# Seven-product row pairs in an fp32 decoder trunk: sums ahead of low parts on VectorE, and four of eight row pairs by seven products in the second MLP matrices and in retention's gates and values

## The chip, the cores and the metric

The kernel runs on one NeuronCore of a Trainium2 chip. The metric is the device time of one execution in microseconds, lower is better. Before the change it was 2503.48 us (median of 3 runs, 2501.48 to 2504.06).

The engines are named as in the profile: PE (TensorE, matrix products), DVE (VectorE, elementwise work), ACT (ScalarE, casts, activations, copies out of PSUM), POOL (GpSimd, here mostly DMA issues), SP (SyncE, here the queue that issues the weight loads). Each runs its own instructions in the order of its own queue and waits for others by semaphores.

## The reference

A trunk of two layers on 256 tokens and a width of 2048, all in float32. Layer 0 is RetNet retention, layer 1 is multi-head latent attention (MLA); each is followed by a squared-ReLU MLP of width 8192.

```python
def retention(h, w_in, w_out, cos, sin):
    proj = h @ w_in
    q, k, v, gate = jnp.split(proj, [H * dk, 2 * H * dk, 2 * H * dk + H * dv], axis=-1)
    ...
    return (jax.nn.silu(gate) * o) @ w_out

def sq_relu_mlp(h, w1, w2):
    return jnp.square(jax.nn.relu(h @ w1)) @ w2

for layer in range(DEPTH):
    if layer < N_A_LAYERS:
        h = rms_norm(x, norm_mix[layer])
        x = x + retention(h, ret_w_in[layer], ret_w_out[layer], ret_cos, ret_sin)
    else:
        ...
        x = x + mla_attention(h, ...)
    x = x + sq_relu_mlp(rms_norm(x, norm_mlp[layer]), mlp_w1[layer], mlp_w2[layer])
```

Weights pass through the core once; nearly all work is products of 256 rows of activations with weight matrices.

## The kernel before, in words

**Split products.** PE multiplies in fp32r, a rounded format. To keep float32 accuracy every operand is split into a high part (the rounded value, a cast on ACT) and a low part (value minus high part, a subtraction on DVE): `split`, lines 183 and 184. A product of two operands is three matmuls into one PSUM bank: high by high (line 352), high by low of the weights (line 353), low by high (line 354).

**Row pairs.** `gemm_pair` multiplies the 256 activation rows by 1024 columns of a weight matrix. It walks over the 2048 contraction rows in eight row pairs of 256 rows, numbered 0 to 7; `quad` does one. One DMA on SP's queue brings 128x2048 elements (1 MB, tile `raw`, three buffers). They are four blocks of 128x512: b11, b22, b12, b21.

- *By eight products.* Two parts of 1024 elements are split; each part feeds four products. That is 24 matmuls, two casts and two subtractions of 1024.
- *By seven products* (the Strassen-Winograd form). Three adds on DVE (lines 312, 316, 317) make four sums of weight blocks in two tiles of 1024 (tag `us`, two buffers). Four parts are split: part 0 (b11 and b22, 1024), part 1 (b21, 512), part 2 (the second sums tile) and part 3 (the first). They feed 2, 1, 2 and 2 products: 21 matmuls. The activations need sums too (`with_sums`): three small operations on DVE and one more split of 512.

High and low parts of the weights live in tiles `wh` and `wl`, five buffers each, so casts and subtractions run at most a few parts ahead of PE.

**Which row pairs go by seven.** `SEVEN = (3, 5, 7)`; `FOUR = (3, 5, 6, 7)` and `QUERY = (3, 4, 6, 7)`. Before the change `FOUR` is used for the second half of MLA's output matrix (`wop`) and `QUERY` for MLA's query matrix (`dqp`). `SEVEN` is used for the first MLP matrices (`u`, without row pair 3 for the very first block), for the second MLP matrices (`d`), for retention's gates and values (`rp`, heads 1 to 7) and its output matrix (`ro`).

**The MLP.** Hidden width 8192 is taken in four groups of 2048. A group is two pairs of calls: two `gemm_pair` for w1 (a *u stage*), then two for w2 (a *d stage*, 1024 output columns each, called its first and second pair here). The result of the second u call is added up, squared, transposed and split while the first d pair already runs: function `up` in `mlp`, lines 778 to 800, which also calls `with_sums` for the hidden blocks whose index is in `SEVEN`. So the d stage's first pair shares its time with that work, and its second pair with `pair_out` of the first (lines 364 to 379) and with POOL's accumulating DMAs into x's home in DRAM (`to_home`, line 148). In each layer's last group the second pair is two plain `gemm` calls instead. That makes eight first pairs and six second pairs.

**Retention.** For heads 1 to 7, two projections (`rq`, `rk`) are followed by one `gemm_pair` (`rp`) for gate and value of the head. Its activations `act0` are the same for all heads; their sums are made once, in `first_inputs` (lines 571 to 586), from the tile `x0t`, which is kept until then.

**Order.** Python code runs once and emits instructions; the `later` list and `tick` decide where deferred work is emitted, and a scheduler then fixes the order of each engine's queue. Dependencies are tracked by tiles.

Of the kernel before, what the change touches and what calls it, by code (L numbers as in the profile page):

```python
# [11 lines left out]
F32 = mybir.dt.float32  # L12
# [3 lines left out]
AF = mybir.ActivationFunctionType  # L16
ALU = mybir.AluOpType
# [49 lines left out]
def yoco(ctx: ExitStack, tc: tile.TileContext, a):  # L67
# [86 lines left out]
    def gain(col):  # L154
        return gains[:, col : col + 1]
# [24 lines left out]
    def split(h, l, src, scale=None):  # L180

        if scale is None:
            nc.scalar.copy(h, src)  # L183
            nc.vector.tensor_tensor(l, src, h.bitcast(F32), op=ALU.subtract)  # L184
        else:
            nc.scalar.activation(h, src, AF.Copy, scale=scale)
            nc.vector.scalar_tensor_tensor(
                l, src, scale, h.bitcast(F32), op0=ALU.mult, op1=ALU.subtract
            )

    def split_act(v, src, scales=(None, None)):
        if scales == (None, None):
# [60 lines left out]
    def gemm_t(w, chunk0, act, nk, name, done):  # L253
# [3 lines left out]
        for g in range(n):  # L257
# [19 lines left out]

            stream(w, chunk0 + g, 2048, f"{name}{g}", use, (lambda: done(acc)) if g == n - 1 else None)

    def quad(w, chunk, x, mm, name):  # L280

        raw = pool.tile([P, 2048], F32, tag="raw", bufs=3, name=f"{name}_raw")
        nc.sync.dma_start(raw, w[chunk])
        v, more = x

        def a(t, k):
            return [v[:, k, i, t * P : (t + 1) * P] for i in range(2)]

        def s(n):
            return [more[:, n // 2, i, n % 2 * P : (n % 2 + 1) * P] for i in range(2)]  # L290

        def parts(src, n, part):
            wh = pool.tile([P, 1024], F32R, tag="wh", bufs=5, name=f"{name}_wh{part}")
            wl = pool.tile([P, 1024], F32R, tag="wl", bufs=5, name=f"{name}_wl{part}")
            split(wh[:, : n * 512], wl[:, : n * 512], src)
            return [[i[:, j * 512 : (j + 1) * 512] for i in (wh, wl)] for j in range(n)]

        if more is None:
            b11, b22 = parts(raw[:, 0:1024], 2, 0)
            mm("c11", a(0, 0), b11)  # L300
            mm("c21", a(1, 0), b11)
            mm("c12", a(0, 1), b22)
            mm("c22", a(1, 1), b22)
            b12, b21 = parts(raw[:, 1024:], 2, 1)
            mm("c12", a(0, 0), b12)
            mm("c22", a(1, 0), b12)
            mm("c11", a(0, 1), b21)
            mm("c21", a(1, 1), b21)
            return
        b11, b22 = parts(raw[:, 0:1024], 2, 0)  # L310
        u = [pool.tile([P, 2, 512], F32, tag="us", bufs=2, name=f"{name}_u{i}") for i in range(2)]
        nc.vector.tensor_tensor(
            u[0], raw[:, 0:1024].rearrange("p (i n) -> p i n", i=2),
            raw[:, 1024:1536].unsqueeze(1).to_broadcast([P, 2, 512]), op=ALU.add,
        )
        nc.vector.tensor_tensor(u[1][:, 0], u[0][:, 0], raw[:, 512:1024], op=ALU.add)
        nc.vector.tensor_tensor(u[1][:, 1], u[1][:, 0], raw[:, 1536:], op=ALU.add)  # L317
        mm("p1", a(0, 0), b11)
        mm("c12", s(3), b22)
        (b21,) = parts(raw[:, 1536:], 1, 1)  # L320
        mm("c11", a(0, 1), b21)
        u2, u4 = parts(u[1].rearrange("p i n -> p (i n)"), 2, 2)
        mm("c21", a(1, 1), u4)
        mm("p6", s(2), u2)
        u1, u3 = parts(u[0].rearrange("p i n -> p (i n)"), 2, 3)
        mm("p5", s(1), u1)
        mm("p7", s(0), u3)
# [243 lines left out]
    def first_inputs(c):  # L571

        t = f2k([2, S], f"x0t_{c}")
        nc.sync.dma_start(t, a["xt"][:, 2 * c : 2 * c + 2, :])
        v = act_tile(f"a0_{c}")
        split_act(v, t, [gain(G_MIX0 + 2 * c + j) for j in range(2)])
        act0.append(v)
        sums0.append(None)
        if c in SEVEN:

            def sum_up():
                for j in range(2):
                    nc.scalar.activation(t[:, j], t[:, j], AF.Copy, scale=gain(G_MIX0 + 2 * c + j))
                sums0[c] = with_sums(t, f"a0s_{c}")

            later(9 + c, sum_up)

# [140 lines left out]
    for h in range(RH):  # L728
        qk, gate, v, s = [], [], [], []
        if h == 0:  # L730

            def gated(acc, gate=gate):
                src = [f2k([512], f"gate_raw{t}") for t in range(NT)]
                for t in range(NT):
                    nc.scalar.copy(src[t], acc[t])

                def silu():
                    for t in range(NT):
                        g = f2k([512], f"gate0{t}")
                        nc.scalar.activation(g, src[t], AF.Silu, scale=r0[t])  # L740
                        gate.append(g)

                later(8, silu)

            gemm(a["ret_w_gv0"], 0, act0, KD, 512, "rg0", gated, start)
            ret_projected(h, qk, gate, v, s)
            gemm(
                a["ret_w_gv0"], 4, act0, KD, 512, "rv0",
                lambda acc, v=v, s=s, gate=gate: ret_valued(acc, 0, s, v, gate),
            )  # L750
            continue

        def paired(c, h=h, gate=gate, v=v, s=s):
            c = summed(c)
            for t in range(NT):
                nc.scalar.activation(c[t][0], c[t][0], AF.Silu, scale=r0[t])
                gate.append(c[t][0])
            ret_valued([c[t][1] for t in range(NT)], h, s, v, gate)

        ret_projected(h, qk, gate, v, s)  # L760
        if h == RH // 2:
            ret_out_half(0)
        need(r0, NT)
        while None in [sums0[k] for k in SEVEN]:
            run_first()
        gemm_pair(a["ret_w_gv"], (h - 1) * 8, list(zip(act0, sums0)), [k in SEVEN for k in range(8)], f"rp{h}", paired)
    ret_out_half(1)


    def mlp(layer, act, r, done):  # L770
        w1, w2 = a[f"mlp_w1_{layer}"], a[f"mlp_w2_{layer}"]
        f0 = 0
        for gi, nf in enumerate(GROUPS):
            hid, blocks = [], []
            kinds = [i in SEVEN for i in range(2 * nf)]
            last = gi == len(GROUPS) - 1

            def up(c, p, hid=hid, blocks=blocks):
# [7 lines left out]
                def turn(i):  # L786
                    for q in (2 * i, 2 * i + 1):
                        name = f"hid{layer}_{p}{q}"
                        tp = transposed(
                            lambda t, j: c[t][q // 2][:, (q % 2 * 2 + j) * P : (q % 2 * 2 + j + 1) * P], f"{name}_tp"  # L790
                        )
                        u = f2k([2, S], f"{name}_u")
                        nc.scalar.activation(u, tp, AF.Square)
                        v = act_tile(name)
                        split_act(v, u)
                        blocks.append((v, with_sums(u, name) if len(blocks) in SEVEN else None))
                        hid.append(v)

                later(0, lambda: turn(0))
# [382 lines left out]
```

## Time and profile before

| | |
|---|---|
| median of 3 runs | 2503.48 us |
| span of the profiled execution, first to last instruction | 2497.0 us |
| PEld (weight load) busy | 2075.1 us, 83% |
| POOL busy | 252.2 us, 10% |
| HBM traffic over the span | 207 GB/s |
| matmuls of `u`, `d`, `rp` from the activations themselves into c banks, on each of lines 352 to 354 | 748, 644, 322 |

The page's own execution spans 2497.0 us; some 6.5 us of the median lie outside of what the profile shows, or between runs. In the page a group's row gives count, busy time, the mean duration of one instruction, and the idle time of its engine just before such instructions with the engine that ended it. A window row gives each engine's busy time in a stretch. Busy time of overlapping instructions is counted once.

### The profile page before, as it was taken

The numbers are of one execution on the slowest core, as the hardware profiler recorded it, in microseconds if no ns is written. First come the engines' busy times: TensorE is split into PE (matmuls) and PEld (weight loads), VectorE is DVE, ScalarE is ACT, GpSimd is POOL, SyncE is SP. The second block draws the span as 40 slices with busy tenths as digits, with TensorE's granted clock in tenths as the row PEclk, the third lists the DMA queues.
The fourth block names the chain that finished last, engine by engine and source line by source line (L and its number), as shares of the span: only waits on it lengthen the run. The fifth ranks groups of instructions, "written<-read, shape, count | busy, mean of one in ns | idle before, by whom it ended". The sixth has DMA issues, their size and how long they took to land.

```text
span 2497.0 us, 31492 instructions
## 1 busy us (share of the span) xinstructions
PE 2471.9 (99%) x11683; PEld 2075.1 (83%) x11683; DVE 2096.7 (84%) x2723; ACT 1574.8 (63%) x2228; POOL 252.2 (10%) x308
## 2 busy tenths in 40 slices
PE   8999999999999999999999999999999999999999
PEld 7788888888888888888888888998888888888887
DVE  7788888888898888889889888776899888898896
ACT  6566555555676657566666767666676566575663
POOL 6300011000010110110110101110010201101100
PEclk9999999999999999999999999999999999999999
DMA  8545568555565685775875555444455956857754
GB/s 290 211 173 202 178 217 246 183 193 196 211 217 189 207 263 186 235 237 186 247 259 191 197 196 189 159 149 163 173 213 203 262 203 213 249 187 233 258 200 165
DMA packets 92825, 519.97 MB, mean 208 GB/s; under 512 B 11009, under 2 KB 12161, under 8 KB 39425
## 3 DMA queue, kind: packets, MB, share of 16 engines
q1 hardware_dynamic: 71280, 471.78, 52.5%
q0 software_dynamic: 21248, 46.15, 8.9%
q8 instruction: 91, 1.49, 0.2%
q14 instruction: 62, 0.50, 0.1%
q10 hardware_dynamic: 144, 0.05, 0.0%
HBM read 478.09 MB, written 39.85 MB: 207 GB/s over the span
## 4 chain that ended last, share of the span: by engine, by line
PE 80%; DVE 10%; DMA 4%; ACT 4%; issue 2%; POOL 1%; ACTq 0%; SPq 0%; DVEq 0%; POOLq 0%
PE u_c L353 7%; PE u_c L354 7%; PE u_c L352 7%; PE d_c L353 4%; PE d_c L354 4%; PE d_c L352 4%; PE rp_c L353 3%; PE rp_c L354 3%; PE rp_c L352 3%; DVE d_wl L184 3%; PE ro_c L352 2%; PE ro_c L353 2%; PE ro_c L354 2%; PE rq_acc L272 2%; PE rk_acc L272 2%; DMA d_raw<-in_mlp_w 2%
## 5 line engine op out<-in xcount | busy, mean ns | idle before, releaser
L184 DVE TENSOR_TENSOR u_wl<-u_raw,u_wh 128x1024 fp32r<-128x1024 f32 (+1 forms) x256 | 280.0, 1124 | 35.8 <-ACT u_wh L183 35.8
L184 DVE TENSOR_TENSOR d_wl<-d_raw,d_wh 128x1024 fp32r<-128x1024 f32 (+1 forms) x256 | 283.4, 1132 | 26.0 <-ACT d_wh L183 25.1
L353 PE MATMUL u_c<-u_wl,n 128*128 128x512 f32 x748 | 291.8, 390 | 1.1 <-DVE u_wl L184 1.0
L352 PE MATMUL u_c<-u_wh,n 128*128 128x512 f32 x748 | 291.3, 391 | 0.0
L354 PE MATMUL u_c<-u_wh,n 128*128 128x512 f32 x748 | 291.3, 389 | 0.0
L183 ACT CAST u_wh<-u_raw 128x1024 fp32r<-128x1024 f32 (+1 forms) x256 | 238.9, 981 | 60.6 <-DMA u_raw<-in_mlp_w 27.2
L183 ACT CAST d_wh<-d_raw 128x1024 fp32r<-128x1024 f32 (+1 forms) x256 | 240.0, 991 | 56.3 <-DMA d_raw<-in_mlp_w 25.1
L353 PE MATMUL d_c<-d_wl,hid 128*128 128x512 f32 x644 | 251.4, 390 | 1.7 <-DVE d_wl L184 1.6
L352 PE MATMUL d_c<-d_wh,hid 128*128 128x512 f32 x644 | 252.1, 391 | 0.0
L354 PE MATMUL d_c<-d_wh,hid 128*128 128x512 f32 x644 | 250.9, 390 | 0.0
L183 ACT CAST u_wh<-u_u 128x1024 fp32r<-128x1024 f32 x92 | 94.2, 1050 | 153.5 <-DVE u_u L317 129.8
L183 ACT CAST d_wh<-d_u 128x1024 fp32r<-128x1024 f32 x84 | 84.9, 1049 | 162.6 <-DVE d_u L317 154.7
L353 PEld LDWEIGHTS u_c<-u_wl,n 128*128 128x128 f32 x748 | 140.5, 188 | 31.1 <-DVE u_wl L184 2.8
L354 PEld LDWEIGHTS u_c<-u_wh,n 128*128 128x128 f32 x748 | 140.4, 188 | 29.2
L352 PEld LDWEIGHTS u_c<-u_wh,n 128*128 128x128 f32 x748 | 140.4, 188 | 28.6
L183 ACT CAST rp_wh<-rp_raw 128x1024 fp32r<-128x1024 f32 x112 | 106.7, 972 | 67.7 <-PE rp_c L354 37.5
L184 DVE TENSOR_TENSOR u_wl<-u_u,u_wh 128x1024 fp32r<-128x1024 f32 x92 | 110.7, 1222 | 43.6 <-ACT u_wh L183 43.5
L353 PEld LDWEIGHTS d_c<-d_wl,hid 128*128 128x128 f32 x644 | 120.9, 188 | 29.0 <-DVE d_wl L184 4.5
L354 PEld LDWEIGHTS d_c<-d_wh,hid 128*128 128x128 f32 x644 | 120.9, 188 | 25.1
L352 PEld LDWEIGHTS d_c<-d_wh,hid 128*128 128x128 f32 x644 | 120.9, 188 | 24.6
L184 DVE TENSOR_TENSOR d_wl<-d_u,d_wh 128x1024 fp32r<-128x1024 f32 x84 | 99.9, 1222 | 35.9 <-ACT d_wh L183 35.9
L148 POOL DMA_DIRECT2D xh<-d_c x48 | 42.1, 1029 | 844.6 <-ACT d_c L369 844.5
(567 smaller groups left out, 6570.0 us busy)
## 6 DMA issues: line engine op xcount, KB each, us to landing
u_raw<-in_mlp_w SPq DMA_DIRECT2D x128, 1024.0 KB, 5.3
d_raw<-in_mlp_w SPq DMA_DIRECT2D x112, 1024.0 KB, 4.9
rp_raw<-in_ret_w_gv SPq DMA_DIRECT2D x56, 1024.0 KB, 4.9
ro_raw<-in_ret_w_out SPq DMA_DIRECT2D x32, 1024.0 KB, 4.9
uq_raw<-in_mla_w_uq SPq DMA_DIRECT2D x24, 768.0 KB, 4.1
rq_raw<-in_ret_w_qk SPq DMA_DIRECT2D x16, 1024.0 KB, 6.6
rk_raw<-in_ret_w_qk SPq DMA_DIRECT2D x16, 1024.0 KB, 4.8
d_raw<-in_mlp_w2t SPq DMA_DIRECT2D x16, 1024.0 KB, 5.1
```

Of the source, the lines that this page charges most:

```text
L148: nc.gpsimd.dma_start(x_home[t][2 * p + j], part, accum_op=ALU.add)
L183: nc.scalar.copy(h, src)
L184: nc.vector.tensor_tensor(l, src, h.bitcast(F32), op=ALU.subtract)
L272: nc.tensor.matmul(acc[f], wh[:, cols], a.rearrange("p i s -> p (i s)"), start=k == 0, stop=k == nk - 1)
L352: nc.tensor.matmul(dst, ah, bh, start=n == 0, stop=False)
L353: nc.tensor.matmul(dst, ah, bl, start=False, stop=False)
L354: nc.tensor.matmul(dst, al, bh, start=False, stop=n == total[key] - 1)
```

## The change

`quad` emits the three adds first and splits part 0 and part 1 afterwards; a new dependency without a semaphore (`queued_behind`) keeps the two subtractions behind the last add in DVE's queue. The d stages' row pairs, the hidden blocks with sums, and retention's `rp` use `FOUR` in place of `SEVEN`. In `first_inputs` the sums of activations are made from a second load of the same rows of x (`again`), and x0t is no longer kept. First MLP matrices, retention's output matrix, `wop` and `dqp` keep their choice of row pairs and get the new order.

```diff
@@ split
         if scale is None:
             nc.scalar.copy(h, src)
-            nc.vector.tensor_tensor(l, src, h.bitcast(F32), op=ALU.subtract)
-        else:
-            nc.scalar.activation(h, src, AF.Copy, scale=scale)
-            nc.vector.scalar_tensor_tensor(
-                l, src, scale, h.bitcast(F32), op0=ALU.mult, op1=ALU.subtract
-            )
+            return nc.vector.tensor_tensor(l, src, h.bitcast(F32), op=ALU.subtract)
+        nc.scalar.activation(h, src, AF.Copy, scale=scale)
+        return nc.vector.scalar_tensor_tensor(
+            l, src, scale, h.bitcast(F32), op0=ALU.mult, op1=ALU.subtract
+        )
@@ new
+    def queued_behind(ins, before):
+        tc.add_manual_dep(
+            ins.ins, before.ins.name,
+            mybir.DependencyInfo(mybir.DependencyClass.NoSync, mybir.DependencyReason.DATA), reason="order",
+        )
@@ quad
-        def parts(src, n, part):
+        def parts(src, n, part, after=None):
...
-            split(wh[:, : n * 512], wl[:, : n * 512], src)
+            low = split(wh[:, : n * 512], wl[:, : n * 512], src)
+            if after is not None:
+                queued_behind(low, after)
...
-        b11, b22 = parts(raw[:, 0:1024], 2, 0)
         u = [pool.tile([P, 2, 512], F32, tag="us", bufs=2, name=f"{name}_u{i}") for i in range(2)]
...
-        nc.vector.tensor_tensor(u[1][:, 1], u[1][:, 0], raw[:, 1536:], op=ALU.add)
+        summed_up = nc.vector.tensor_tensor(u[1][:, 1], u[1][:, 0], raw[:, 1536:], op=ALU.add)
+        b11, b22 = parts(raw[:, 0:1024], 2, 0, summed_up)
         mm("p1", a(0, 0), b11)
         mm("c12", s(3), b22)
-        (b21,) = parts(raw[:, 1536:], 1, 1)
+        (b21,) = parts(raw[:, 1536:], 1, 1, summed_up)
@@ first_inputs
-        if c in SEVEN:
+        if c in FOUR:
 
             def sum_up():
+                again = f2k([2, S], f"x0s_{c}")
+                nc.sync.dma_start(again, a["xt"][:, 2 * c : 2 * c + 2, :])
                 for j in range(2):
-                    nc.scalar.activation(t[:, j], t[:, j], AF.Copy, scale=gain(G_MIX0 + 2 * c + j))
-                sums0[c] = with_sums(t, f"a0s_{c}")
+                    nc.scalar.activation(again[:, j], again[:, j], AF.Copy, scale=gain(G_MIX0 + 2 * c + j))
+                sums0[c] = with_sums(again, f"a0s_{c}")
@@ the loop over heads
-        while None in [sums0[k] for k in SEVEN]:
+        while None in [sums0[k] for k in FOUR]:
             run_first()
-        gemm_pair(a["ret_w_gv"], (h - 1) * 8, list(zip(act0, sums0)), [k in SEVEN for k in range(8)], f"rp{h}", paired)
+        gemm_pair(a["ret_w_gv"], (h - 1) * 8, list(zip(act0, sums0)), [k in FOUR for k in range(8)], f"rp{h}", paired)
@@ mlp
-            kinds = [i in SEVEN for i in range(2 * nf)]
+            kinds = [i in FOUR for i in range(2 * nf)]
...
-                        blocks.append((v, with_sums(u, name) if len(blocks) in SEVEN else None))
+                        blocks.append((v, with_sums(u, name) if len(blocks) in FOUR else None))
```

## The prediction

> **What bounds the kernel now.** I read the page first, then the windows view (busy time by stage), the groups with shapes kept apart, and the timelines of DVE and PE inside one d stage.
>
> ```profile
> span 2497.0 us, 31492 instructions
> PE 2471.9 (99%) x11683; PEld 2075.1 (83%) x11683; DVE 2096.7 (84%) x2723; ACT 1574.8 (63%) x2228; POOL 252.2 (10%) x308
> ```
>
> PE is busy throughout; DVE has 400 us free, but the free time counts only where it lies. The stages (first pair of a d stage, three of eight alike; its second pair, two of six; a u stage; one `rp`; the `wop` call, which already takes four row pairs by seven):
>
> ```profile
> core 0: us, PE busy (x) PEld busy (x) DVE busy (x) ACT busy (x) POOL busy (x), PEclk, DMA share, GB/s
> 820.90:864.40 43.50, 43.49 (x201) 35.95 (x200) 39.88 (x50) 29.76 (x43) 2.15 (x4) 1.00 0.58 198
> 991.10:1034.60 43.50, 43.50 (x200) 35.94 (x199) 39.89 (x50) 29.74 (x43) 1.93 (x3) 1.00 0.57 198
> 2404.60:2447.90 43.30, 43.30 (x199) 35.77 (x198) 40.50 (x52) 29.56 (x42) 0.00 (x0) 1.00 0.56 195
> 1034.60:1076.50 41.90, 41.87 (x185) 34.28 (x185) 35.02 (x36) 25.00 (x31) 7.71 (x10) 1.00 0.87 255
> 2277.50:2319.60 42.10, 41.72 (x184) 34.24 (x183) 35.03 (x36) 24.88 (x31) 7.62 (x10) 1.00 0.87 254
> 906.40:991.10 84.70, 84.70 (x383) 70.32 (x382) 73.89 (x82) 53.72 (x69) 4.33 (x5) 1.00 0.66 220
> 244.40:287.30 42.90, 42.90 (x193) 35.61 (x192) 35.08 (x45) 24.48 (x31) 0.00 (x0) 1.00 0.49 180
> 1762.50:1804.60 42.10, 42.10 (x191) 34.56 (x189) 37.55 (x47) 27.12 (x40) 0.96 (x2) 1.00 0.54 188
> ```
>
> PE sets every stage. But in a first pair DVE works 39.9 of 43.5 us, because the last hidden blocks are made there too. Its idle 3.6 us are waits of its own, in DVE's timeline of the d stage at 991 (start, time, instruction, idle before):
>
> ```profile
> 991.31 0.69 DVE L385 TENSOR_TENSOR u_c<-u_c,u_p 128x512 f32<-128x512 f32 x1 [0.23 <-ACT u_p L369]
> 997.39 2.35 DVE L184 TENSOR_TENSOR d_wl<-d_raw,d_wh 128x1024 fp32r<-128x1024 f32 x2
> 999.66 0.42 DVE L392 TENSOR_TENSOR hid_sum<-hid_u 128x256 f32<-128x256 f32 x1
> 999.99 1.28 DVE L184 TENSOR_TENSOR hid<-hid_u,hid 128x512 fp32r<-128x512 f32 x2
> 1001.20 0.28 DVE L393 TENSOR_TENSOR hid_sum<-hid_sum,hid_u 128x128 f32<-128x128 f32 x1
> 1001.40 1.22 DVE L184 TENSOR_TENSOR d_wl<-d_raw,d_wh 128x1024 fp32r<-128x1024 f32 x1
> 1009.76 1.23 DVE L184 TENSOR_TENSOR d_wl<-d_u,d_wh 128x1024 fp32r<-128x1024 f32 x1 [0.32 <-ACT d_wh L183]
> 1020.38 2.36 DVE L184 TENSOR_TENSOR d_wl<-d_u,d_wh 128x1024 fp32r<-128x1024 f32 x2 [1.19 <-ACT d_wh L183]
> 1030.41 2.36 DVE L184 TENSOR_TENSOR d_wl<-d_u,d_wh 128x1024 fp32r<-128x1024 f32 x2 [1.20 <-ACT d_wh L183]
> 1032.80 1.23 DVE L184 TENSOR_TENSOR d_wl<-d_raw,d_wh 128x1024 fp32r<-128x1024 f32 x1
> ```
>
> The three waits of 0.32, 1.19 and 1.20 us stand in row pairs 3, 5 and 7: the last add is done, ACT casts the sums, DVE stands. And PE is close behind. Its timeline, first uses of a low part in row pairs 3 and 4 and at the end of 7:
>
> ```profile
> 1009.71 0.39 PE L353 MATMUL d_p<-d_wl,hid 128*128 128x512 f32 x1
> 1014.47 0.39 PE L353 MATMUL d_c<-d_wl,hid 128*128 128x512 f32 x1
> 1033.51 0.39 PE L353 MATMUL d_p<-d_wl,hid_more 128*128 128x512 f32 x1
> ```
>
> DVE ends row pair 7's last part at 1030.41+2.36 = 1032.77; PE wants it at 1033.51. The reserve is 0.74 us: a first pair is balanced between two engines.
>
> **What PE saves.** A row pair by seven takes 1014.47-1009.71 = 4.76 us for 21 matmuls, 0.227 us each. The change makes 14 `d` calls and 7 `rp` calls take one more row pair by seven, three matmuls less each: 63 x 0.227 = 14.3 us if PE stays the bound, 0.68 us a call.
>
> **What DVE pays.** The groups with shapes (count, busy, mean ns):
>
> ```profile
> L184 DVE TENSOR_TENSOR d_wl<-d_raw,d_wh 128x1024 fp32r<-128x1024 f32 x214 | 254.6, 1220 | 26.0 <-ACT d_wh L183 25.1
> L312 DVE TENSOR_TENSOR d_u<-d_raw 128x1024 f32<-128x1024 f32 x42 | 51.2, 1220 | 2.3 <-DMA d_raw<-in_mlp_w 2.3
> L317 DVE TENSOR_TENSOR d_u<-d_u,d_raw 128x512 f32<-128x512 f32 x42 | 28.9, 688 | 0.8
> L184 DVE TENSOR_TENSOR hid_more<-hid_sum,hid_more 128x512 fp32r<-128x512 f32 x24 | 16.4, 685 | 0.0
> ```
>
> Instructions overlap, so I price them start to start from the timeline above: 1024 elements (999.66-997.39)/2 = 1.135 us; 512: (1001.20-999.99)/2 = 0.605; 256: 0.33; 128: 0.20. Row pair 6 by eight is two of 1024; by seven it is four of 1024 and three of 512. More by 2 x 1.135 + 3 x 0.605 = 4.085 us. In a first pair hidden block 6 also needs sums: 0.33 + 2 x 0.20 + 0.605 = 1.335 us. (Block 6 comes from the second u call, so it falls just there.) Together 5.42 us.
>
> A rule of the Trainium skill speaks against the change more strongly: VectorE: DVE Perf Modes, The DRAIN you can't avoid, says that the next operation starts only when the pipe has emptied. Priced by the whole times of these rows, 1.22, 0.69, 0.42, 0.28 and 0.68 us, the extra would be 6.17 us, and the forecast some 6 us later. Here the trace disagrees: the operation after 997.39+2.35 = 999.74 starts at 999.66.
>
> **What the new order gives.** Adds now stand first, and the subtractions of parts 0 and 1 (1.135 + 0.605 = 1.74 us) stand between the last add and the subtraction of its sums. ACT's cast with its handover took 1.19 us, so these waits close: 0.32 + 1.19 + 1.20 = 2.71 us in a first pair. If ACT were held up by something else in its queue, that cover is gone and 1.19 us per row pair return.
>
> **First pairs, the sum.** DVE cannot begin earlier: at 991.31 it waits for ACT's copy of the u call's finished product, and from there its queue is full to row pair 7. The end of row pair 7's last part moves from 1032.77 by +5.42-2.71 to 1035.48. PE, with three matmuls less, wants it at 1033.51-0.68 = 1032.83. So PE stands 2.65 us, 0.06 more by handover, and the pair gets 2.7-0.7 = 2.0 us longer. Bounds: no less than 1.8 (DVE's 39.9+5.4 = 45.3 us against 43.5, with no idle at all), no more than 3.2 (a bubble of 0.3 as at 1009.76 in each of four row pairs). I take 2.0, eight times: +16 us.
>
> **Second pairs.** DVE has 35.0+4.1 = 39.1 us of work in 42.0-0.7 = 41.3, so PE should save its 0.68 us. But DMA is busy to 0.87 there (POOL's accumulating DMAs beside the loads), and row pair 5's load is late:
>
> ```profile
> d_raw<-in_mlp_w SPq DMA_DIRECT2D x112, 1024.0 KB, 4.9
> ```
>
> ```profile
> d_raw<-in_mlp_w SPq DMA_DIRECT2D x5, 1024.0 KB, 8.0
> ```
>
> ```profile
> 1053.00 1.23 DVE L312 TENSOR_TENSOR d_u<-d_raw 128x1024 f32<-128x1024 f32 x1 [0.28 <-DMA d_raw<-in_mlp_w]
> 1054.87 3.49 DVE L184 TENSOR_TENSOR d_wl<-d_raw,d_wh 128x1024 fp32r<-128x1024 f32 x3
> ```
>
> ```profile
> 1055.73 0.39 PE L352 MATMUL d_c<-d_wh,hid 128*128 128x512 f32 x1
> 1056.15 0.50 PE L353 MATMUL d_c<-d_wl,hid 128*128 128x512 f32 x1
> ```
>
> (The first row is a load's median time to landing over the run, the second that in the window 1036 to 1060; then DVE's and PE's timelines.) The scheduler puts row pair 5's adds ahead of row pair 4's subtractions, they wait for the load, and PE waits 0.19 us beyond its step at 1055.73. In the changed program's order this grows: row pair 5's first add stands even before row pair 3's last subtraction, and all three adds before row pair 4's. If the load lands 2.0 us later like everything else, at 1055.0, row pair 4's part is ready at 1055.0 + 3 x 1.135 + 2 x 0.605 = 1059.6, and PE wants it at 1055.96+2.0: 1.6 us late, which is +0.8 for the pair. If the load keeps its time, the pair gains 0.68+0.19 = 0.9. Ends -0.9 and +0.8; I take 0, since neither end is nearer to a row: 0 +-5 us for six.
>
> **Retention.** DVE has 35.1+4.1 = 39.2 us of work in 42.9-0.7 = 42.2. That is 93%, where `wop` shows 89% at PE's pace, but `wop` still has the old order's waits, which close here; PE should keep up. Seven calls: -4.8 us; at worst nothing. The first call also makes one more sum (1.3 us) and four more loads of 256 KB pass through SP's queue between the weight loads; I put 0 on it, -1 to +3. The new order in u stages, `ro`, `wop` and `dqp` gives nothing: PE is busy there already (84.70 of 84.70).
>
> **Sum.** +16 + 0 - 4.8 = +11 us on a span of 2497.0. The median stands 6.5 us above that span; I carry the difference over: 2503.5 + 11 = 2515 us, 0.45% slower.
>
> **Rivals.** (a) *PE stays the bound*: all 63 matmuls are saved, -14.3 us, 2489. For it: DVE's overall 84%, and `wop` with four row pairs by seven at PE's pace. Against: `wop` has 37.55 us of DVE work, a first pair would have 45.3. It decides if DVE's added work in a first pair stays under the 3.6 us that are idle. (b) *The loads decide*: row pair 5's DMA holds DVE's queue in every second pair, and ACT's bubbles stay: first pairs +2.8, second +0.8, retention -4.8: +22, 2526. The share of 0.87 speaks for it; the stall of only 0.19 now against. (c) *No change to speak of*: the earlier sums in the u stage let DVE enter the first pair ahead, a first pair costs 1.0, second pairs gain 0.9: +8 - 5 - 5 = -2, 2501. Against it stands the wait at 991.31, which no reserve removes. (d) *Stalls slow the clock.* PE idle of 1.88 us was followed by a lower granted clock:
>
> ```profile
> 1640.24 0.66 PE L203 MATMUL qptp<-cst,qpp 128*128 128x128 f32 x4 [1.88 <-DVE ot L184]
> ```
>
> ```profile
> 1640.00:1652.00 12.00, 11.76 (x69) 11.70 (x70) 10.15 (x32) 7.00 (x15) 2.31 (x1) 0.86 0.36 135
> ```
>
> At 0.86, 12 us lose 1.7; eight first pairs would lose 14 more: 2529. The first pair's 2.7 us do not fall in one piece. Before row pair 3's first part the changed queue holds, from 1001.40+1.135 on, two of 1024 (that part included), six of 512, two of 256 and five of 128 elements: 7.6 us, so it is ready at 1010.1 against 1009.71, 0.4 late. From row pair 5 on each takes DVE 4 x 1.135 + 3 x 0.605 = 6.36 us and PE 4.76, so at most 1.6 fall between two of them, short of 1.88. The Trainium skill, TensorE: Matmul & The Clock Gate, part 1, asks for an idle window of about 3.4 us; the trace drops sooner than that, so the row and not the page sets this rival.
>
> **Chances.** Forecast 0.57, its own range 2507 to 2523; (a) 0.07; (b) 0.22; (c) 0.11; (d) 0.03. 0.2% (5 us) is what a measurement of this kernel can tell from no change. Faster 0.07, same 0.12 (c and the low edge of the forecast), slower 0.81. The range 2506 to 2530 takes in the forecast's bounds and (b), and leaves out (a) and (c).
>
> **What would show it.** Right: first pairs of 45 to 46 us with DVE busy nearly throughout, PE idle before row pair 7 released by DVE's line 184; no waits of 1.2 us before subtractions of sums; `rp` windows 0.7 us shorter. Wrong: first pairs at 42.8 (rival a), second pairs at 43 or more with DVE waiting for DMA (b), a granted clock under 1.00 in a d stage (d).

## The result and the profile after

The changed kernel takes 2514.12 us (median of 4 runs, 2513.54 to 2517.25); the kernel before, on the same chip, 2502.48 us (2498.68 to 2504.06). The ratio is 1.0057, 95% interval 1.004 to 1.0075: about 12 us slower. The forecast was 2515.

First the page of the changed kernel: span, then busy time of the engines.

```profile
span 2512.1 us, 31602 instructions
...
PE 2463.6 (98%) x11620; PEld 2056.5 (82%) x11620; DVE 2190.2 (87%) x2864; ACT 1630.7 (65%) x2281; POOL 251.7 (10%) x308
```

PE makes 63 matmuls less, and DVE works 93 us more than before (2190.2 against 2096.7). Where that lies, the windows of the changed kernel show (busy time by stage, columns as in the prediction): a first pair, its second pair, a second pair of the other layer, a u stage, one `rp`, `wop`.

```profile
987.60:1033.20 45.60, 43.52 (x197) 35.00 (x196) 45.11 (x59) 32.19 (x45) 2.42 (x4) 1.00 0.56 184
1033.20:1077.80 44.60, 41.77 (x181) 33.48 (x181) 38.83 (x41) 26.23 (x32) 6.87 (x10) 1.00 0.83 242
2288.10:2331.90 43.80, 41.73 (x181) 33.43 (x180) 38.84 (x41) 26.06 (x32) 6.80 (x10) 1.00 0.83 245
902.80:987.60 84.80, 84.80 (x384) 70.37 (x383) 74.27 (x84) 55.67 (x71) 4.69 (x6) 1.00 0.68 221
239.10:281.30 42.20, 42.20 (x190) 34.93 (x189) 38.94 (x49) 25.80 (x32) 0.00 (x0) 1.00 0.52 185
1764.70:1806.50 41.80, 41.80 (x191) 34.61 (x190) 38.37 (x47) 28.33 (x42) 0.90 (x2) 1.00 0.54 187
```

A first pair grew from 43.5 to 45.6 us, and DVE is busy in 45.11 of them, PE in 43.52. A second pair grew from 42 to 44, although DVE has 5 to 6 us free there. `rp` fell from 42.9 to 42.2.

To hundredths I measure a call from its first matmul with a low part to that of the next call. By that the eight first pairs cost +18.1 us, the six second pairs +11.5, the seven `rp` calls -3.7; the rest, -10.8, is spread over the program's start and the calls outside of the d stages. Together +15.1, the difference of the two spans; that is one execution of each kernel, and the medians differ by 11.6.

DVE's timeline in the first pair at 987.6: its first wait, row pairs 6 and 7, and the end.

```profile
987.41 0.69 DVE L392 TENSOR_TENSOR u_c<-u_c,u_p 128x512 f32<-128x512 f32 x1 [0.23 <-ACT u_p L376]
...
1018.54 1.22 DVE L318 TENSOR_TENSOR d_u<-d_raw 128x1024 f32<-128x1024 f32 x1
1019.79 0.69 DVE L322 TENSOR_TENSOR d_u<-d_u,d_raw 128x512 f32<-128x512 f32 x1
1020.52 0.69 DVE L323 TENSOR_TENSOR d_u<-d_u,d_raw 128x512 f32<-128x512 f32 x1
...
1025.14 1.22 DVE L318 TENSOR_TENSOR d_u<-d_raw 128x1024 f32<-128x1024 f32 x1
...
1027.12 0.69 DVE L323 TENSOR_TENSOR d_u<-d_u,d_raw 128x512 f32<-128x512 f32 x1
1027.73 1.82 DVE L184 TENSOR_TENSOR d_wl<-d_raw,d_wh 128x1024 fp32r<-128x1024 f32 x2
1029.47 2.35 DVE L184 TENSOR_TENSOR d_wl<-d_u,d_wh 128x1024 fp32r<-128x1024 f32 x2
```

No wait is left between these rows. The three waits of 0.32, 1.19 and 1.20 us before subtractions of sums are gone, in the whole program too: the group of these subtractions has no idle time before it.

```profile
L184 DVE TENSOR_TENSOR d_wl<-d_u,d_wh 128x1024 fp32r<-128x1024 f32 x112 | 133.2, 1217 | 0.0
```

Now PE's timeline in the same pair: in row pair 6 and again in row pair 7 three matmuls of high parts run, and the fourth waits for the high part of the sums. Below it ACT's cast in row pair 7.

```profile
1021.51 0.39 PE L359 MATMUL d_c<-d_wh,hid 128*128 128x512 f32 x1
1022.42 0.50 PE L359 MATMUL d_c<-d_wh,hid 128*128 128x512 f32 x1 [0.53 <-ACT d_wh L183]
...
1027.10 0.39 PE L359 MATMUL d_c<-d_wh,hid 128*128 128x512 f32 x1
1029.02 0.50 PE L359 MATMUL d_c<-d_wh,hid 128*128 128x512 f32 x1 [1.53 <-ACT d_wh L183]
```

```profile
1027.92 2.00 ACT L183 CAST d_wh<-d_u 128x1024 fp32r<-128x1024 f32 x2 [3.13 <-DVE d_u L323]
```

PE normally starts a matmul every 0.227 us. Here it loses 1022.42 - 1021.51 - 0.23 = 0.68 us and 1029.02 - 1027.10 - 0.23 = 1.69 us. Its releaser is ACT's cast of the sums; in row pair 7 ACT in turn stood 3.13 us until DVE's last add (1027.12 + 0.69 = 1027.81). So the delay there is DVE's, handed on by ACT. In row pair 6 the trace puts ACT's wait down to a matmul that frees a buffer, but DVE's last add ends at the same time (1020.52 + 0.69 = 1021.21; the cast starts at 1021.33), so it does not tell the two apart; e8 and e9 do.

Last a second pair, DVE and then PE, in the changed kernel.

```profile
1048.07 1.22 DVE L184 TENSOR_TENSOR d_wl<-d_u,d_wh 128x1024 fp32r<-128x1024 f32 x1
1052.44 1.23 DVE L318 TENSOR_TENSOR d_u<-d_raw 128x1024 f32<-128x1024 f32 x1 [3.16 <-DMA d_raw<-in_mlp_w]
1053.59 1.22 DVE L184 TENSOR_TENSOR d_wl<-d_u,d_wh 128x1024 fp32r<-128x1024 f32 x1
```

```profile
1054.86 0.50 PE L360 MATMUL d_p<-d_wl,hid_more 128*128 128x512 f32 x1 [1.44 <-DVE d_wl L184]
...
1057.45 0.50 PE L360 MATMUL d_c<-d_wl,hid 128*128 128x512 f32 x1 [0.93 <-DVE d_wl L184]
```

DVE stands 3.16 us with row pair 5's first add, which waits for its load. Behind that add stand row pair 3's last subtraction (1053.59) and all of row pair 4's, and PE waits for both. The loss that is left, 0.6 us, is one more wait for DVE in row pair 7.

### The profile page after: what moved, and what is told of

Read it like the earlier page. It is cut to its first block, busy times and chain, and to the rows that moved or that the text cites. A ratio compares the mean times of both kernels' runs of the same rounds, so it can differ in the third digit from the quotient of the medians.

```text
span 2512.1 us, 31602 instructions
## 1 busy us (share of the span) xinstructions
PE 2463.6 (98%) x11620; PEld 2056.5 (82%) x11620; DVE 2190.2 (87%) x2864; ACT 1630.7 (65%) x2281; POOL 251.7 (10%) x308
## 4 chain that ended last, share of the span: by engine, by line
PE 69%; DVE 21%; issue 3%; DMA 3%; ACT 2%; POOL 0%; SPq 0%; DVEq 0%; ACTq 0%; POOLq 0%
DVE d_wl L184 9%; PE u_c L360 7%; PE u_c L361 7%; PE u_c L359 7%; DMA d_raw<-in_mlp_w 2%; DVE d_u L318 2%; PE rp_c L359 2%; PE rp_c L361 2%; PE rp_c L360 2%; PE rq_acc L271 2%; PE rk_acc L271 2%; PE ro_c L360 2%; PE ro_c L359 2%; PE ro_c L361 2%; PE u_p L360 1%
## 5 line engine op out<-in xcount | busy, mean ns | idle before, releaser
L184 DVE TENSOR_TENSOR d_wl<-d_raw,d_wh 128x1024 fp32r<-128x1024 f32 (+1 forms) x256 | 273.2, 1101 | 26.6 <-ACT d_wh L183 26.6
L359 PE MATMUL d_c<-d_wh,hid 128*128 128x512 f32 x560 | 221.5, 395 | 17.0 <-ACT d_wh L183 17.0
L360 PE MATMUL d_c<-d_wl,hid 128*128 128x512 f32 x560 | 219.5, 392 | 5.5 <-DVE d_wl L184 5.5
L361 PE MATMUL d_c<-d_wh,hid 128*128 128x512 f32 x560 | 218.3, 390 | 0.0
L183 ACT CAST d_wh<-d_u 128x1024 fp32r<-128x1024 f32 x112 | 113.3, 1048 | 134.2 <-DVE d_u L323 88.0
L359 PEld LDWEIGHTS d_c<-d_wh,hid 128*128 128x128 f32 x560 | 105.1, 188 | 45.0 <-ACT d_wh L183 23.8
L184 DVE TENSOR_TENSOR d_wl<-d_u,d_wh 128x1024 fp32r<-128x1024 f32 x112 | 133.2, 1217 | 0.0
L360 PEld LDWEIGHTS d_c<-d_wl,hid 128*128 128x128 f32 x560 | 105.1, 188 | 32.4 <-DVE d_wl L184 10.8
L148 POOL DMA_DIRECT2D xh<-d_c x48 | 42.1, 1026 | 881.9 <-ACT d_c L376 881.7
L361 PEld LDWEIGHTS d_c<-d_wh,hid 128*128 128x128 f32 x560 | 105.2, 188 | 21.2
```

The source lines that it names most:

```text
L148: nc.gpsimd.dma_start(x_home[t][2 * p + j], part, accum_op=ALU.add)
L184: return nc.vector.tensor_tensor(l, src, h.bitcast(F32), op=ALU.subtract)
L359: nc.tensor.matmul(dst, ah, bh, start=n == 0, stop=False)
L360: nc.tensor.matmul(dst, ah, bl, start=False, stop=False)
L361: nc.tensor.matmul(dst, al, bh, start=False, stop=n == total[key] - 1)
```

## The experiments

Each kernel ran beside the kernel before on one chip. The ratio is to that; its interval is at 95%. The groups e1 to e4, e5 to e7, e8 to e11 and e12 ran on four different chips, so kernels of different groups are compared by their ratios.

| kernel | median us | before there | ratio | interval |
|---|---|---|---|---|
| after (the change) | 2514.12 | 2502.48 | 1.0057 | 1.0040-1.0075 |
| e1 new order only | 2485.41 | 2500.89 | 0.9939 | 0.9924-0.9954 |
| e2 choice only | 2572.54 | 2500.89 | 1.0289 | 1.0272-1.0306 |
| e3 second load only | 2495.68 | 2500.89 | 0.9981 | 0.9971-0.9991 |
| e4 all but the d stages' choice | 2478.74 | 2500.89 | 0.9913 | 0.9898-0.9928 |
| e5 after, adds queued behind | 2514.27 | 2496.98 | 1.0071 | 1.0049-1.0093 |
| e6 e4, four in second pairs | 2497.91 | 2496.98 | 1.0002 | 0.9992-1.0012 |
| e7 after, hidden sums on POOL | 2545.95 | 2496.98 | 1.0193 | 1.0171-1.0215 |
| e8 after, two adds more | 2525.54 | 2501.49 | 1.0096 | 1.0081-1.0111 |
| e9 after, one cast more | 2517.46 | 2501.49 | 1.0066 | 1.0041-1.0090 |
| e10 after, no accumulating DMAs | 2496.64 | 2501.49 | 0.9983 | 0.9974-0.9993 |
| e11 e4, four in first pairs | 2519.50 | 2501.49 | 1.0076 | 1.0059-1.0092 |
| e12 after, sums home later | 2509.83 | 2496.37 | 1.0053 | 1.0036-1.0070 |

### The change taken apart: e1 to e4

**e1** is the changed kernel with the old choice of row pairs and the old sums of activations; only `quad`'s order is new.

```diff
-        if c in FOUR:
+        if c in SEVEN:
...
-        gemm_pair(a["ret_w_gv"], (h - 1) * 8, list(zip(act0, sums0)), [k in FOUR for k in range(8)], f"rp{h}", paired)
+        gemm_pair(a["ret_w_gv"], (h - 1) * 8, list(zip(act0, sums0)), [k in SEVEN for k in range(8)], f"rp{h}", paired)
...
-            kinds = [i in FOUR for i in range(2 * nf)]
+            kinds = [i in SEVEN for i in range(2 * nf)]
```

> The new order alone, with SEVEN in the d stages and in rp as before. Theory (the order closes DVE's waits for ACT's casts, and nothing there was on the path in u, d and ro; where it shortened dqp, wop, uq and wo in the changed kernel, by 1.4 + 1.4 + 1.6 + 0.9 us, it does so here too): first pairs stay at 43.5 us, no wait of 1.19 us before a subtraction of sums, the whole some 5 us faster than before, 2497. Rival (those 5 us come from elsewhere or from chance): dqp 43.9 and wop 43.1 as before, the whole within 2 us of before.

Measured: 0.9939, 15 us faster, more than the theory gave it. First pairs went from 43.52 to 43.28, second pairs from 42.1 to 41.5, `dqp` from 43.88 to 42.53, `wop` from 43.10 to 41.76, `uq` from 132.81 to 131.23, `wo` from 64.85 to 63.94. `uq` and `wo` hold no row pairs, and their part is not of the order: the granted clock of their windows is 0.99 and 0.95 in the execution before, 1.00 and 0.97 in e1's, and e2, in the old order, has `uq` at 131.23 too. The second `u` call of every stage (43.28) and all four `ro` calls kept their time to 0.01, and so did four of the seven `rp` calls. Its first pair's window and its page have

```profile
988.20:1031.50 43.30, 43.30 (x201) 36.04 (x200) 40.72 (x51) 31.82 (x43) 2.67 (x4) 1.00 0.63 202
...
PE 2463.0 (99%) x11683; PEld 2074.7 (84%) x11683; DVE 2096.2 (84%) x2723; ACT 1598.7 (64%) x2228; POOL 245.5 (10%) x308
```

The same 11683 matmuls as before are busy for 2463.0 us and not for 2471.9. Of these 8.9 us, 2.5 are `uq` and `wo` with their clock; the rest was counted as busy before and was no work. A first pair shows it plainly: the same matmuls fill 43.50 of 43.50 us before and 43.30 of 43.30 here.

**e2** is the kernel before with the new choice and the second load, in the old order.

```diff
-            kinds = [i in SEVEN for i in range(2 * nf)]
+            kinds = [i in FOUR for i in range(2 * nf)]
...
-        if c in SEVEN:
+        if c in FOUR:
```

> FOUR in the d stages and in rp, with the old order. Theory (a first pair lasts as long as DVE's queue): the queue holds 5.42 us more and one more wait of 1.19 us, row pair 7's last part is ready 6.5 us after PE wants it, so a first pair takes 43.5 + 5.9 = 49.4 us; eight of them +47 us, the whole 2545 to 2565. Rival (the order does not matter in first pairs, PE waits for casts or buffers): first pairs of 45.7 us as in the changed kernel, the whole 2510 to 2520.

Measured: 1.0289, 72 us slower, above the theory's range; the rival falls. Its window of a first pair:

```profile
1005.70:1056.60 50.90, 46.86 (x198) 35.96 (x198) 45.30 (x59) 33.98 (x48) 3.45 (x4) 0.97 0.57 178
```

DVE has nearly the same work as in the changed kernel (45.30 us against 45.11), but the pair takes 50.9: the casts' waits stay, 1.17 to 1.19 us before the subtractions of sums in row pairs 5 to 7. PE's longer stalls, of 1.75 and 1.73 us in this pair, come with a granted clock of 0.97. So the order is worth 15 us with three row pairs by seven, and about 60 us with four (72 against 12).

**e3** is the kernel before with the sums of activations taken from a second load.

```diff
+                again = f2k([2, S], f"x0s_{c}")
+                nc.sync.dma_start(again, a["xt"][:, 2 * c : 2 * c + 2, :])
...
-                sums0[c] = with_sums(t, f"a0s_{c}")
+                sums0[c] = with_sums(again, f"a0s_{c}")
```

> The kernel before, with the second load of x's rows for the sums of activations in place of keeping the first tile, and nothing else. Theory (three buffers kept until the sums are made held up the start: in the changed kernel the first projection is 3.2 us and head 1's first projection with what stands in it 3.2 us shorter): the first rp starts 4 to 5 us earlier than at 106.9, the whole 4 to 5 us faster, 2498. Rival (the start varies from run to run): the first rp within 1 us of 106.9 and the whole within 2 us of before.

Measured: 0.9981, 5 us faster. In the trace head 1's `rq` fell from 17.28 to 13.95 us and its `rk` rose from 12.16 to 13.70, 1.8 us gained. The rest is not settled: the first matrix of the program took between 24.3 and 27.3 us in the profiled executions of kernels with the second load, 26.1 in e1 and 27.6 before, which have none.

**e4** is the changed kernel with three row pairs by seven in the d stages.

```diff
-            kinds = [i in FOUR for i in range(2 * nf)]
+            kinds = [i in SEVEN for i in range(2 * nf)]
...
-                        blocks.append((v, with_sums(u, name) if len(blocks) in FOUR else None))
+                        blocks.append((v, with_sums(u, name) if len(blocks) in SEVEN else None))
```

> The whole change without the d stages: new order, second load, FOUR in rp, SEVEN in the d stages. Theory (all of the loss is in the d stages; rp saves 0.64 us a call, the start 4.5 us, the order 5 us): rp of 42.2 us, first pairs of 43.5 and second pairs of 42.0 as before, the whole 2486 to 2492. Rival (the loss is spread, DVE's larger share delays other stages too): above 2495.

Measured: 0.9913, 22 us faster than the kernel before and some 36 us faster than the changed one by the ratios. The 2478.74 us lie below the theory's 2486 to 2492; e1 shows where most of that comes from, as the order gave 15 us and not the 5 put on it. It is the fastest version here. Windows of a first and a second pair:

```profile
981.90:1025.20 43.30, 43.30 (x201) 36.04 (x200) 40.74 (x51) 31.83 (x43) 2.65 (x4) 1.00 0.62 202
1025.20:1066.70 41.50, 41.50 (x185) 34.38 (x184) 34.14 (x35) 24.19 (x29) 7.01 (x9) 1.00 0.88 255
```

All that the change loses lies in the d stages' fourth row pair.

### What sets a first pair: e7, e8, e9

**e8** lengthens DVE's queue alone, **e9** ACT's alone.

```diff
         summed_up = nc.vector.tensor_tensor(u[1][:, 1], u[1][:, 0], raw[:, 1536:], op=ALU.add)
+        if name[0] == "d" and name[-2:] == "06":
+            for i in range(2):
+                summed_up = nc.vector.tensor_tensor(u[1][:, 1], u[1][:, 0], raw[:, 1536:], op=ALU.add)
```

> The changed kernel, with VectorE's last add of row pair 6 in each of the eight first pairs of the d stages made three times in place of once (the same values again), and nothing else. An add that waits for the one before starts about 0.73 us after it, so VectorE gets 1.45 us more in each first pair. Theory (VectorE's queue is as long as the first pair): first pairs go from 45.65 to 47.1, the whole by 8 x 1.45 = 11.6 us to about 2526. Rival (ScalarE's casts or the buffers set the pace, VectorE is full only beside them): first pairs 45.65 to 46.2, at most 2519.

```diff
+            if name[0] == "d" and name[-2:] == "06" and part == 0:
+                nc.scalar.copy(wh[:, : n * 512], src)
             low = split(wh[:, : n * 512], wl[:, : n * 512], src)
```

> The counterpart of e8 on ScalarE: the cast of the first part of row pair 6 in each first pair is made twice, 0.96 to 1.15 us more of ScalarE each. Theory (VectorE's queue sets the end, ScalarE waits for it): first pairs stay within 0.3 of 45.65, 2514 to 2517. Rival (ScalarE's own queue sets it): first pairs 46.6 or more, 2522 or more.

The first pair's window of e8, then that of e9:

```profile
988.60:1035.80 47.20, 43.73 (x198) 35.06 (x197) 46.56 (x61) 32.30 (x45) 2.51 (x4) 1.00 0.54 180
```

```profile
988.70:1034.40 45.70, 43.66 (x198) 35.06 (x197) 45.12 (x59) 33.21 (x46) 2.52 (x4) 1.00 0.56 185
```

Two adds more on DVE lengthen a first pair by 1.46 us (45.65 to 47.11 in the first of them), the whole price of 2 x 0.73; with a cast more on ACT the eight take what they took, within 0.05. DVE's queue sets a first pair; ACT's queue, though the trace names ACT as the releaser, has room for one more cast. (The added cast stands ahead of the sums' own; a longer cast of the sums, in series behind DVE's last add, was not tried.) The medians, 2525.5 and 2517.5, follow; the runs of e9 spread from 2511.7 to 2525.5, so its verdict rests on the trace.

**e7** was to shorten DVE's queue.

```diff
-                        blocks.append((v, with_sums(u, name) if len(blocks) in FOUR else None))
+                        blocks.append((v, with_sums(u, name, nc.gpsimd) if len(blocks) in FOUR else None))
```

> The changed kernel, with the three small operations that form the sums of the hidden blocks on POOL and not on VectorE. In a first pair three or four blocks' sums fall there: 0.73 us of VectorE each, 2.2 us or more. Theory (the length of a first pair is the length of VectorE's queue): first pairs go from 45.65 to about 43.5, second pairs stay at 43.3-44.6, about 2497 us. Rival (ScalarE's casts in their own queue, or their buffers, hold TensorE, and VectorE is full only beside that): first pairs stay at 45.6, 2514. If POOL's results come late, the sums of blocks 3, 5, 6, 7 are late and first pairs are longer than 45.65.

It failed: 1.0193, first pairs of 49.0 us. POOL's group of the first sums, and DVE's timeline beside it:

```profile
L401 POOL TENSOR_TENSOR hid_sum<-hid_u 128x256 f32<-128x256 f32 x32 | 56.3, 1760 | 628.8 <-ACT hid_u L804 628.8
```

```profile
1005.78 0.69 DVE L322 TENSOR_TENSOR d_u<-d_u,d_raw 128x512 f32<-128x512 f32 x1
1006.50 1.11 DVE L323 TENSOR_TENSOR d_u<-d_u,d_raw 128x512 f32<-128x512 f32 x1
1007.54 1.48 DVE L184 TENSOR_TENSOR d_wl<-d_raw,d_wh 128x1024 fp32r<-128x1024 f32 x1
```

The first sum takes 1.76 us on POOL, 0.42 on DVE; and while POOL works (from 1005.93), DVE's own add takes 1.11 us in place of 0.69. PE stood 3.40 us in one piece in row pair 3: the low part that it wanted stood on DVE behind a subtraction whose sums came late. So e7 says nothing on its question; e8 and e9 answer it.

### What sets a second pair: e5, e6, e10, e11, e12

**e5** takes the late load's add out of the way of finished work.

```diff
-        nc.vector.tensor_tensor(
+        first_add = nc.vector.tensor_tensor(
...
+        if name[0] == "d" and name[-2] == "1":
+            queued_behind(first_add, last_low[0])
```

> The changed kernel, with one edit: in a second pair of a d stage each row pair's first add stands on VectorE behind the last subtraction of the row pair before it, so that an add that waits for its load has no finished work behind it. Theory (the late load holds VectorE's queue): the six second pairs go from 43.3-44.6 us to 41-42, about 2.3 us each, first pairs stay at 45.65: about 2500 us. Rival (VectorE's four more microseconds of work limit the second pairs, wherever they wait): second pairs stay at 43.5-44.5 and the time at 2514. Second rival (the order of after made the adds early on purpose; behind the subtractions ACT's casts of the sums come late): second pairs above 44.6, over 2515.

**e6** is e4 with this order and with four row pairs in the second pairs alone.

```diff
-            kinds = [i in SEVEN for i in range(2 * nf)]
+            kinds = [[i in choice for i in range(2 * nf)] for choice in (SEVEN, FOUR)]
```

> New order, reload and four row pairs in the retention calls as in e4 (2478.7 us), and in the d stages four row pairs by seven in the second pairs alone, with the adds behind the last subtraction as in e5; first pairs take three by seven but still make the sums of hidden block 6, as the second pair needs them. Theory: a first pair has 3.6 + 2.7 us of VectorE to spare for the 1.3 us of sums and stays at 43.3; second pairs lose 0.68 us each against e4's 41.48, 40.8: about 2475. Rival (loads or VectorE keep the second pairs): second pairs 41.5 or more, first pairs 43.3 to 44.6: 2479 to 2490.

Windows of the second pair and the u call behind it, e5 and then e6:

```profile
1034.80:1076.30 41.50, 41.20 (x182) 33.64 (x181) 38.04 (x40) 25.59 (x31) 7.05 (x10) 1.00 0.87 255
1076.30:1120.40 44.10, 42.21 (x185) 34.11 (x184) 35.28 (x37) 25.07 (x30) 4.49 (x6) 1.00 0.77 236
```

```profile
1030.70:1072.10 41.40, 41.09 (x182) 33.71 (x181) 37.03 (x39) 24.73 (x30) 6.84 (x9) 1.00 0.86 250
1072.10:1116.70 44.60, 42.08 (x185) 34.08 (x184) 35.33 (x37) 25.03 (x30) 4.51 (x6) 1.00 0.77 233
```

Second pairs fell to 41.4-41.5 us as expected, and the u call that follows rose from 41.5 to 43.9-44.6, once to 47.7. The stall had moved, and the totals did not come down (e6 is some 22 us slower than e4 by the ratios): the theory was right of the stage and wrong of the program. That u call also runs beside accumulating DMAs, those of the second pair. e6's first pairs took 43.70, 0.42 more than e4's, for the sums of hidden block 6.

**e10** leaves out the accumulating DMAs.

```diff
-                    into_x(done, c, p) if last else to_home(c, p)
+                    if last:
+                        into_x(done, c, p)
```

> The changed kernel without the accumulating DMAs that bring the d stages' sums home, in the six d stages that are not the last of a layer (eight transfers for each pair of columns, 96 in all; the output lacks these sums). The arithmetic on all engines and its order stay as they are. Theory (the loads of a second pair are late because they share the DMA engines with these transfers, and VectorE's queue then stands): second pairs go from 43.3-44.6 us to about 40.8, first pairs stay at 45.65, the whole falls by 6 x 3.2 = 19 us to about 2495. Rival (four microseconds more of VectorE's work are too many for a second pair by themselves): second pairs stay at 43 or more, 2505 to 2514.

**e11** gives the fourth row pair to the first pairs alone.

```diff
-            kinds = [i in SEVEN for i in range(2 * nf)]
+            kinds = [[i in choice for i in range(2 * nf)] for choice in (FOUR, SEVEN)]
```

> The counterpart of e6: as e4 (2478.7 us), with four row pairs by seven in the first pairs of the d stages alone; the second pairs keep three, and nothing is queued otherwise than in e4. Theory (a first pair's loss is its own VectorE work): first pairs 45.65 against 43.28, second pairs 41.5 as in e4: 2478.7 + 8 x 2.37 = 2498. Rival (a first pair that uses up VectorE's lead hands its delay on): second pairs 42.5 or more, 2504 or more.

The second pair's window of e10, then that of e11:

```profile
1031.30:1072.20 40.90, 40.90 (x181) 33.61 (x181) 39.06 (x41) 26.36 (x31) 0.00 (x0) 1.00 0.60 210
```

```profile
1032.40:1076.50 44.10, 42.15 (x184) 34.12 (x184) 35.15 (x36) 25.10 (x30) 7.17 (x10) 1.00 0.85 245
```

In e10 DVE does all its 39.06 us of work within 40.9, and PE does not stall; the total falls to 2496.6, as expected. DVE's work is not too much for a second pair. In e11, against my theory, the second pairs take 43.3-44.5 us with only three row pairs by seven, where e4's take 41.5 with the same work. The difference comes in from the first pair. This is DVE and PE at the second part of row pair 0 of the second pair: in e4, then in e11.

```profile
1023.53 1.23 DVE L184 TENSOR_TENSOR d_wl<-d_raw,d_wh 128x1024 fp32r<-128x1024 f32 x1 [0.57 <-ACT d_wh L183]
...
1028.11 0.39 PE L360 MATMUL d_c<-d_wl,hid 128*128 128x512 f32 x1
```

```profile
1034.05 1.22 DVE L184 TENSOR_TENSOR d_wl<-d_raw,d_wh 128x1024 fp32r<-128x1024 f32 x1
...
1035.39 0.42 PE L360 MATMUL d_c<-d_wl,hid 128*128 128x512 f32 x1
```

In e4 DVE is 3.35 us ahead of PE, in e11 0.12. DVE's progress also frees the load buffers: row pair 5's load is issued 7.4 us into the pair in e4 (1032.60) and 8.6 us in e11 (1041.04). Row pair 5's add therefore waits for its load until 1040.44 in e4, 15.2 us into the pair, and until 1051.20 in e11, 18.8 us in.

```profile
1040.44 1.23 DVE L318 TENSOR_TENSOR d_u<-d_raw 128x1024 f32<-128x1024 f32 x1 [1.84 <-DMA d_raw<-in_mlp_w]
```

```profile
1051.20 1.23 DVE L318 TENSOR_TENSOR d_u<-d_raw 128x1024 f32<-128x1024 f32 x1 [2.82 <-DMA d_raw<-in_mlp_w]
```

The kernel before had no such lead either. The same place there, DVE and then PE:

```profile
1035.68 1.23 DVE L184 TENSOR_TENSOR d_wl<-d_raw,d_wh 128x1024 fp32r<-128x1024 f32 x1
...
1037.59 0.39 PE L353 MATMUL d_c<-d_wl,hid 128*128 128x512 f32 x1
```

DVE is 0.68 us ahead, and row pair 5's add waits until 18.4 us into the pair (1053.00, in the prediction); in the changed kernel until 19.2 (1052.44). So against the kernel before, the load is only 0.8 us later. Most of what is lost beyond that comes from what stands behind the waiting add: before, one more add and then row pair 4's part, ready 3.0 us after the load's add started (1054.87 + 1.135 - 1053.00); after, row pair 3's last subtraction and two adds stand between, and it is ready 4.9 us after (1056.18 + 1.135 - 1052.44). e5 shows this by cause: its load lands as late, 18.8 us into the pair (1053.67 of a pair that starts at 1034.85), but no finished work stands behind the add, and the pair takes 41.5.

**e12** tried to give the load its old place ahead of the transfers.

```diff
-        later(1, rest)
+        later(3 if name[0] == "d" and name[-2:] in ("00", "10", "20") else 1, rest)
```

> The changed kernel, with the last part of a first pair's output (two subtractions, then the four accumulating DMAs of its second columns) emitted two row pairs later, in the six d stages that are not the last of a layer. In the trace of e11 (same first pairs) these four DMAs were issued from 1037.86 to 1040.71, the load of row pair 5 behind them at 1041.04, and it took 10.1 us; in e4's, where VectorE is ahead of TensorE, that load was issued at 1032.60, ahead of all four (1033.24 to 1036.37), and took 7.7 us. Theory (a late VectorE frees the load's buffer late, and the load then falls behind the four transfers): with them moved behind it the load of row pair 5 lands about 2.3 us earlier in the pair, second pairs take 41.5-42.5 us in place of 43.3-44.6, and the whole about 2502 to 2507. Rival (the transfers collide with a load wherever they are, as in e5, where the stall moved into the next u stage): the loads of row pairs 6 and 7 or the next u stage lose what row pair 5 gains, 2510 to 2516.

Second pairs took 42.9-43.4 us, 5.6 us less over six than in the changed kernel, about half of what the theory asked. The ratio, 1.0053, is not told apart from 1.0057. The four transfers were now issued from 1037.66 to 1044.34, the load at 1039.38 between them, and it still took 10.5 us. That the transfers delay the loads is shown by e10; whether their order decides stays open.

## Why the prediction came out right, and where it did not

**PE's saving: right.** `rp` calls lost 0.64 us against 0.68 forecast; the seven together 3.7 against 4.8, as the first and the last gave less. With the transfers gone (e10) a second pair takes 40.92 against e4's 41.48.

**DVE's price in a first pair: right.** From its first wait to the end of row pair 7's last part DVE took 1031.82 - 987.41 = 44.41 us; before, 1032.77 - 991.31 = 41.46. That is +2.95, forecast 5.42 - 2.71 = +2.71. The missing 0.24 is in the three adds: each needs the one before, and they start 1.25 and 0.73 us apart (1018.54, 1019.79, 1020.52) where I priced 1.135 and 0.605. A row pair takes DVE 1025.14 - 1018.54 = 6.60 us, and not 6.36. The prediction read the Trainium skill, VectorE: DVE Perf Modes, The DRAIN you can't avoid, as a rule for every operation; the same section adds that a next operation that is not held (made to wait until all earlier ones have finished) starts earlier. The trace agrees with that: 1027.73 + 1.82 = 1029.55, and the next subtraction, which uses no result of the one before, starts at 1029.47. In these rows only the adds, which use the result before them, start after its end.

**First pairs +2.0 each: right.** Six took +2.12 to +2.17, the two of the last groups +2.6: 18.1 in all, forecast 16. e8 shows by cause that the pair is as long as DVE's queue. Off was where PE stands: I had it wait for row pair 7's last low part on DVE. It waits within row pairs 6 and 7, for ACT's cast of the sums; e8 and e9 show that ACT hands DVE's delay on.

**The waits of 1.2 us close: right**, as the group without idle time shows, and e2 shows what they cost where the cover is missing.

**Second pairs 0: wrong, +11.5 for six.** The step that failed is the range of -0.9 to +0.8 with 0 taken. I had found the place (row pair 5's add ahead of row pair 4's subtractions), but let PE's need move by the same 2.0 us as the load and put the part 1.6 us late. Measured from the start of the pair, it was ready at 1057.4 - 1033.2 = 24.2 us, against 1059.6 - 1036.6 = 23.0 in my sum and 1055.96 - 1034.6 = 21.4 needed: 2.8 late. Of the 1.2 us between, 0.8 is the load, which I let land at the same place in the pair as before (18.4 us in, measured 19.2), and the rest is adds that wait for one another. Taking 0 was then a choice of the middle that no row bore out: the load did not keep its time, and no pair gained. What I left out is that a first pair with no idle time hands on no lead, so that the buffers come free late and the loads start late beside the transfers (e11, e10), while the new order puts more finished work behind the load (e5). This was rival (b)'s mechanism, larger than I had it there, and one of the prediction's own signs of being wrong came: second pairs at 43 or more with DVE waiting for DMA. The rival's other half, ACT's waits, did not come.

**The new order gives nothing elsewhere: right in the second `u` calls and in `ro`, wrong in `wop` and `dqp`; in all it gives some 8 us that the sum did not have.** I read a PE that is busy throughout (84.70 of 84.70) as a PE at its pace. Between the profiled executions e1 gained 2497.0 - 2482.6 = 14.4 us; the first pairs' 0.24 x 8 = 1.9, 1.5 at the program's start and the 2.5 of `uq` and `wo`, which go with their clock, leave 8.5. In `wop` and `dqp` together it gained 2.7, in second pairs 3.5, in the plain calls that follow the last groups' first pairs 2.1. The Trainium skill, Perfetto Trace Analysis, Tensor Engine Instruction (MATMUL, LD_WEIGHTS), says that a matmul's end in the profile is an estimate; the trace agrees: a first pair was busy in 43.50 of 43.50 us before and in 43.30 of 43.30 in e1, with the same matmuls. The second load, put at 0 with -1 to +3, gained 5 (interval 2 to 7).

**The sum: right by two errors that cancel.** +11.5 in the second pairs was missing, and a gain of the same size in the other calls. Of that gain, 2.5 us are the clock in `uq` and `wo` and 3.2 the first matrix, which varies nearly as much from execution to execution, so part of it is luck. A third error helps: I carried 6.5 us from span to median. In the changed kernel's profiled run they are 1.8 apart (2513.88 against 2512.1), so the execution profiled before was a quick one; the span, forecast at 2508, came out at 2512.1. Rival (a), that PE stays the bound, fell on the first pairs; (c) fell with them, as no reserve came from the earlier sums; (d) did not come either: the granted clock was 1.00 in these stages, and PE's longest stall in a first pair was 1.69 us.

## What to carry to other kernels

Price a choice between engines by stage: the order, the second load and the retention calls give 22 us (e4), and the same trick in the d stages, whose first pairs leave the second engine no slack, takes some 36 back. An engine that runs ahead carries the loads with it; work that uses up its lead costs again in the next stage, and a repair there can move the stall one stage on (e5, e6), so look at the stage behind before counting a gain. To see whether PE has anything to lose, read the starts of its matmuls, not its busy time.

## What the hardware showed that was not expected

POOL's elementwise work slows DVE's: in e7 DVE had 9 instructions less in a first pair and was busy for 44.86 us against 45.11, as single instructions grew from 0.69 to 1.11 and from 1.22 to 1.48 us beside POOL's. The Trainium skill, SBUF — State Buffer, SBUF: two separate sides, says that the two share one pair of ports as an exclusive lock, where VectorE's operation has two SBUF inputs and GpSimd's reads SBUF. These rows agree that such operations slow each other; that one blocks the other for its whole length they do not show.

Stalls well under 2 us can go with a lower granted clock: in e2's first pair PE stands idle for 1.75 and 1.73 us, 7.7 us apart, and the pair's clock is 0.97; in the changed kernel's first pair it stands idle for 0.53 and 1.53 us, and the clock is 1.00.

A load of 1 MB that takes 4.9 us by the median takes 10.1 beside four accumulating transfers, in e11; those four, of 256 KB each, take 8.2 to 14.8.
